# Pass by pass: the order of TensorE's products in a split-precision decoder trunk

## The chip, the cores and the metric

The kernel runs on one core of one Trainium2 chip. The metric is the device time of one execution in microseconds, as the median of several runs; less is better. The engines are named as in the profile: PE is TensorE's matmul stream, PEld its loading of weights, DVE, ACT and POOL are the vector, scalar and GpSimd engines, SP issues the transfers.

## The reference, cut to what matters

The input x has 256 tokens of width 1024. Two layers follow each other, and every large product is one of these lines:

```python
def swiglu(h, w_gate, w_up, w_down):
    return (jax.nn.silu(h @ w_gate) * (h @ w_up)) @ w_down        # 1024 -> 2816 -> 1024

# layer 0: half-step SwiGLU, Mamba-2 mixer, half-step SwiGLU
x = x + 0.5 * swiglu(rmsnorm(x, norm_w[0, 0]), w_gate[0, 0], w_up[0, 0], w_down[0, 0])
x = x + mamba2_mixer(rmsnorm(x, norm_w[0, 1]), ...)   # h @ w_in (1024 -> 5152), scan, y @ w_out (2048 -> 1024)
x = x + 0.5 * swiglu(rmsnorm(x, norm_w[0, 2]), w_gate[0, 1], w_up[0, 1], w_down[0, 1])
# shared keys and values from the stream after layer 0
k, v = hkv @ w_k + b_k, hkv @ w_v + b_v
# layer 1: half-step SwiGLU, windowed attention over k and v, half-step SwiGLU, final norm
x = x + 0.5 * swiglu(...)
x = x + swa_sink_attention(h, k_rot, v, w_q, b_q, sinks, w_o, b_o, cos, sin)
x = x + 0.5 * swiglu(...)
return rmsnorm(x, final_norm_w)
```

## The kernel before, in words

All weights are cut into **units** of 128 x 1024 numbers, stored in HBM in the order of use and loaded two at a time (one chunk, 1 MB) into a ring of four chunks. For each unit ACT rounds the raw weights to a high part `hi` (L144) and DVE takes the rest as a low part `lo` (L155); `Weights.ahead` keeps four units cut in advance of the one that PE uses. Activations are split in the same way: `xh` and `xl` lie side by side in one tile `xs[k]` for each of the eight row tiles k of 128 rows; a feed-forward's hidden tile is split into `hh` and `hl`. A product is then three products: high weights with high activations, high weights with low activations, and low weights with high activations.

PE runs six stages one after the other: feed-forward (0,0), the mixer, feed-forward (0,1), feed-forward (1,0), attention, feed-forward (1,1). The order of instructions on every engine is written out by hand in `run`, `ffn`, `ssm` and `att`, with a list of slots (`Slots`) for the work that goes between two units. A feed-forward takes gate f, up f and, from f = 4 on, down f - 4; the four last down units stand at its end, the last two of them merged in `tail`.

Three helpers put a unit on PE:

- `wide` (L362 in the profile; gate `g_f` and up `u_f` of a feed-forward, 22 of each for each of the four) takes 512 columns (`xh` and `xl` together) against `hi`, and 256 columns (`xh`) against `lo`: 16 matmuls for a unit. Either the two kinds alternate, row tile by row tile ("alternating" below), or, with `by_part`, all eight wide ones stand ahead of all eight narrow ones ("pass by pass"). Before the change the feed-forwards (0,1) and (1,0) run pass by pass from f = 1 on, (0,0) and (1,1) alternate, and f = 0 alternates everywhere.
- `rows` (L382; down `da_f`, the mixer's output `sa`, attention's output `aa`) makes three matmuls of 256 columns for each of eight output tiles: 24 for a unit. `high_first` chooses between the orders high-high, high-low, low-high (in the down products of (0,1) and (1,0), without the last two) and high-high, low-high, high-low (elsewhere; the first letter is the weight's part).
- `unit` (L349; the first gate, the mixer's inputs `sb`, keys `kab`, queries `q`) makes 24 matmuls of 256 columns, three for each row tile in turn. The very first gate and the mixer's 16 x units are written pass by pass instead: high-high, low-high, high-low, eight row tiles each.

The mixer's 41 input units stand in the order dt, then for each of four groups B, C and x and z in turn. The key units kA and kB stand in feed-forward (1,0) behind f = 5.

Of the kernel before, what the change touches and what calls it, by code (L numbers as in the profile page):

```python
# [17 lines left out]
T = 256  # L18
D = 1024
KT = D // P  # L20
# [195 lines left out]
class Trunk:  # L216
# [119 lines left out]
        nc.scalar.copy(rs, b[:, 0:256])  # L336
        return rs

    def unit(self, what, out, xh=None, xl=None, before=None):

        nc = self.nc
        xh = self.xh if xh is None else xh
        xl = self.xl if xl is None else xl
        hi, lo = self.W.next(what)
        passes = [(k, w, x) for k in range(KT) for w, x in ((hi, xh), (hi, xl), (lo, xh))]
        if self.W.pos == 1 or what[0] == "x":
            passes = [(k, w, x) for w, x in ((hi, xh), (lo, xh), (hi, xl)) for k in range(KT)]
        for n, (k, w, x) in enumerate(passes):
            nc.tensor.matmul(out, w[:, k * P : (k + 1) * P], x[k], start=n == 0, stop=n == len(passes) - 1)  # L349
        if before:  # L350
            before()
        self.tick()
# [16 lines left out]
        self.slots.run()  # L369
        self.W.ahead(self.NPART - 2)  # L370

    def rows(self, units, accs, first, last, done=None, high_first=False):

        nc = self.nc
        for j in range(KT):
            out = accs[j % 4][:, (j // 4) * T : (j // 4) * T + T]
            s = slice(j * P, (j + 1) * P)
            for n, ((hi, lo), hh, hl) in enumerate(units):
                f, e = first and n == 0, last and n == len(units) - 1
                passes = ((hi, hh), (hi, hl), (lo, hh)) if high_first else ((hi, hh), (lo, hh), (hi, hl))  # L380
                for m, (w, x) in enumerate(passes):
                    nc.tensor.matmul(  # L382
                        out, w[:, s], x, start=f and j < 4 and m == 0, stop=e and m == 2, skip_group_check=True
                    )
            if done:
                done(j, out)
# [90 lines left out]
    def ffn(self, l, i, key, nxt):  # L477
        nc, wk = self.nc, self.fw
        self.stage_norm(key)
        accs = self.accs(f"da_{key}")  # L480
        hs = {}

        def evac(f, g, u):
            hh = self.op.tile([P, T], F32R, tag="high", name=f"hh_{key}_{f}")
            hl = self.op.tile([P, T], F32R, tag="low", name=f"hl_{key}_{f}")
            hs[f] = (hh, hl)

            def e0():
                nc.vector.tensor_tensor(g, g, self.rs, ALU.mult)
                nc.scalar.activation(g, g, AF.Silu)  # L490
                nc.vector.tensor_tensor(u, u, self.rs, ALU.mult)

            def e1():
                nc.vector.tensor_tensor(u, u, g, ALU.mult)
                nc.scalar.activation(hh, u, AF.Copy)

            def e2():
                nc.vector.tensor_tensor(hl, u, hh.bitcast(F32), ALU.subtract)

            wait = max(0, 4 - f) if key == "f0" else 2 if f == 0 else 0  # L500
            self.slots.chain(wait, [e0, e1, e2])

        def product(name, f, t):

            b = self.bank(f"{name}_{key}_{f}")
            if self.W.pos == 0:
                self.slots.at(0, lambda: nc.scalar.copy(t, b[:, 0:T]))
                self.unit((name, l, i, f), b[:, 0:T])
                return

            def add():
                nc.scalar.copy(t, b[:, T:])  # L512
                nc.vector.tensor_tensor(t, b[:, 0:T], t, ALU.add)  # L513

            self.slots.at(0, add)
            self.wide((name, l, i, f), b, by_part=l != i and f > 0)

        for f in range(NF):
            g, u = (wk.tile([P, T], F32, tag=n, bufs=4, name=f"{n}s_{key}_{f}") for n in "gu")
            product("g", f, g)  # L520
            evac_now = lambda: evac(f, g, u)
            self.slots.late(0, evac_now)
            product("u", f, u)
            if l == 1 and i == 0 and f == 0:
                self.split_k()
            if l == 1 and i == 0 and f == 5:
                self.shared_k()
            if f >= LAG:
                self.down(l, i, f - LAG, hs, accs)
        for f in range(NF - LAG, NF - 2):  # L530
            self.down(l, i, f, hs, accs)
        self.tail([(("d", l, i, f), *hs.pop(f)) for f in (NF - 2, NF - 1)], accs, nxt)

    def down(self, l, i, f, hs, accs):
        hi_lo = self.W.next(("d", l, i, f))
        hh, hl = hs.pop(f)
        self.rows([(hi_lo, hh, hl)], accs, f == 0, False, high_first=l != i)
        self.tick()

    def tail(self, units, accs, nxt):  # L540
# [7 lines left out]
    def ssm(self, nxt):  # L548
# [9 lines left out]
        accs = []  # L558
# [11 lines left out]
        def half():  # L570
            if st["n"] % 2 == 0:
                st["bank"] = self.bank(f"sb{st['n']}")
            o = st["bank"][:, (st["n"] % 2) * T : (st["n"] % 2) * T + T]
            st["n"] += 1
            return o

        def conv(c, out, o, d):
            u = ubufs[st["u"] % 4]
            st["u"] += 1

            def c0():
                V.tensor_tensor(u[:, 3:], o, self.rs, ALU.mult)

            def c1():
                A.activation(out, u[:, 3:], AF.Identity, scale=self.s("convw", 3 * 24 + c), bias=self.s("convb", c))

            def c2():
                pairs = st["taps"]
                pairs.append((out, u, c))
                if len(pairs) == 1:  # L590
                    sl.late(0, taps)

            def c3():
                A.activation(out, out, AF.Silu)

            sl.chain(d, [c0, c1, c2, c3])
# [168 lines left out]
        def evac(what, o, d):  # L765
            kind = what[0]
            if kind == "dt":
                dt_chain(o, d)
            elif kind == "z":
                zs[what[1]] = z = wk.tile([P, T], F32, tag="zs", bufs=16, name=f"zs{what[1]}")  # L770
                sl.at(d, lambda: V.tensor_tensor(z, o, self.rs, ALU.mult))
                sl.at(d + 1, lambda: A.activation(z, z, AF.Silu))
            elif kind == "x":
                xs[what[1]] = x = wk.tile([P, T], F32, tag="xs", bufs=8, name=f"xs{what[1]}")
                conv(what[1], x, o, d)
            else:
                t = wk.tile([P, T], F32, tag=kind, name=f"{kind}{what[1]}")
                (B if kind == "B" else C)[what[1]] = t
                conv((16 if kind == "B" else 20) + what[1], t, o, d)
# [3 lines left out]
        at = {w: n for n, w in enumerate(seq)}  # L783
        ins = [w for w in seq if w[0] != "so"]

        E = {w: max(3, at[ins[min(i | 1, len(ins) - 1)]] + 1) for i, w in enumerate(ins)}
# [11 lines left out]
        for g in range(GROUPS):  # L798
# [7 lines left out]
            last = max(max(ymm_at[t // 2] + 1, E["z", t] + 2) for t in range(4 * g, 4 * g + 4))  # L806
# [8 lines left out]
            done = last + 3 + NORM_AT[g] + SCALE_AT[g]  # L815
# [7 lines left out]
        for what in seq[:-2]:  # L823
            if what[0] == "so":
                tt = what[1]
                if not accs:
                    accs = self.accs("sa")
                self.rows([(self.W.next(what), yh[tt], yl[tt])], accs, tt == 0, False)
                self.tick()
            else:  # L830
                o = half()
                self.unit(what, o, before=lambda: evac(what, o, E[what] - at[what]))
        self.tail([(w, yh[w[1]], yl[w[1]]) for w in seq[-2:]], accs, nxt)


# [69 lines left out]
    def att(self, nxt):  # L905
# [124 lines left out]
        for j in range(4):  # L1030
            if j == 3:
                vb = self.bank("vps")
                self.shared_v(0, vb)
                sl.at(0, lambda: vdone(vb))
                self.shared_v(1, vb)
            b = self.bank(f"q{j}")
            self.unit(("qA", j), b[:, 0:T])
            Q[j] = [wk.tile([P, T], F32, tag=f"Q{r}", name=f"Q{j}_{r}") for r in range(2)]

            def q_rope(j=j, b=b):  # L1040
                self.rope(b, self.rs, self.s("bq", 2 * j), self.s("bq", 2 * j + 1), "cosq", "sinq", Q[j], f"q{j}")

            d = 2 if j == 0 else 1
            sl.at(d, q_rope)
            d += 2
            sl.late(d, lambda j=j: scores(j))
            d += (4, 3, 3, 1)[j]
            sl.late(d, lambda j=j: turn(j))
            d += (0, 2, 2, 0)[j]
            sl.late(d, lambda j=j: pv(j))  # L1050
            self.unit(("qB", j), b[:, T:])
        accs = self.accs("aa")
# [182 lines left out]
```

## Time and profile before

| what | value |
|---|---|
| median of 3 runs | 1048.29 us (1047.95 to 1049.29) |
| time of the profiled execution | 1048.69 us |
| its span, first to last instruction | 1046.9 us |
| PE busy | 1025.2 us, 98% of the span |
| DVE, ACT, POOL busy | 775.1, 627.7, 79.4 us |
| matmuls, and weight loads | 7290 each |
| feed-forward (0,0), 7.30 to 201.70 | 194.40 us |
| mixer, 201.70 to 398.50 | 196.80 us |
| feed-forward (0,1), 398.50 to 581.60 | 183.10 us |
| feed-forward (1,0), 581.60 to 770.70, with the keys | 189.10 us |
| attention, 770.70 to 846.50 | 75.80 us |
| feed-forward (1,1) and the end, 846.50 to 1046.90 | 200.40 us |

PE is busy nearly all the time, but the profile's matmuls overlap, so that a busy PE can still be a slow one. What counts is the distance from one matmul's start to the next one's. The time of the execution is 1.8 us above the span.

### The profile page before, as it was taken

How to read it: one execution, taken by the hardware profiler on the slowest of the kernel's cores; microseconds unless marked ns; L12 is line 12 of the kernel's file. 1: busy time of each engine (PE TensorE's matmuls, PEld its weight loads, DVE VectorE, ACT ScalarE, POOL GpSimd, SP SyncE). 2: the span in 40 equal slices, each digit the busy share in tenths (PEclk: the TensorE clock that was granted, in tenths of full speed). 3: DMA queues.
4: the chain of work that ended last, by engine and by line, in shares of the span. 5: the costliest groups of instructions: out<-in, count | busy, mean ns of one | idle time of the engine just before them, and what ended most of it. 6: DMA issues, size and time to landing. Idle time of an engine off the chain costs nothing.

```text
span 1046.9 us, 18340 instructions
## 1 busy us (share of the span) xinstructions
PE 1025.2 (98%) x7290; PEld 948.2 (91%) x7290; DVE 775.1 (74%) x1420; ACT 627.7 (60%) x1106; POOL 79.4 (8%) x122
## 2 busy tenths in 40 slices
PE   8999999999999999999999999999999999999996
PEld 7899999999989898999999899999998888999996
DVE  4766666788999977766667796666689777666664
ACT  6555555669877756555555664555565766555554
POOL 3000000210110112000000200000031020000000
PEclk9999999999999999999999999999999999999998
DMA  8555554546545354555455455554554244555521
GB/s 304 195 201 176 186 200 164 194 171 252 217 156 213 131 201 153 197 201 200 169 203 200 157 211 200 177 209 178 202 202 152 92 161 167 196 186 191 187 101 40
DMA packets 30132, 190.84 MB, mean 182 GB/s; under 512 B 3904, under 2 KB 5728, under 8 KB 8544
## 3 DMA queue, kind: packets, MB, share of 16 engines
q1 hardware_dynamic: 30048, 189.69, 51.0%
q8 instruction: 57, 0.93, 0.4%
q14 instruction: 27, 0.22, 0.1%
HBM read 187.27 MB, written 1.10 MB: 180 GB/s over the span
## 4 chain that ended last, share of the span: by engine, by line
PE 80%; DVE 11%; ACT 3%; DMA 2%; POOL 1%; issue 1%; SPq 0%; ACTq 0%; DVEq 0%; POOLq 0%
PE u_f L362 23%; PE g_f L362 22%; PE da_f L382 22%; PE sa L382 3%; PE sb L349 3%; DVE lo L155 2%; DVE xs L394 2%; DMA csb<-cs_scratch 2%; PE aa L382 1%; PE q L349 1%; DVE xs L601 1%; DVE X L402 1%; DMA raw<-w 1%; DVE E L723 1%; ACT hi L144 1%
## 5 line engine op out<-in xcount | busy, mean ns | idle before, releaser
L155 DVE TENSOR_TENSOR lo<-raw,hi 128x1024 fp32r<-128x1024 f32 (+1 forms) x343 | 415.2, 1214 | 15.0 <-ACT hi L144 15.0
L144 ACT ACTIVATE hi<-raw 128x1024 fp32r<-128x1024 f32 (+1 forms) x343 | 357.3, 1047 | 18.9 <-PE da_f L382 5.1
L362 PE MATMUL u_f<-xs,hi 128*128 128x512 f32 x704 | 218.1, 397 | 0.0
L362 PE MATMUL g_f<-xs,hi 128*128 128x512 f32 x696 | 213.7, 395 | 0.8 <-DVE xs L394 0.8
L382 PE MATMUL da_f<-hh_f,hi 128*128 128x256 f32 x704 | 195.8, 278 | 0.0
L382 PE MATMUL da_f<-hh_f,lo 128*128 128x256 f32 x704 | 195.6, 278 | 0.0
L382 PE MATMUL da_f<-hl_f,hi 128*128 128x256 f32 x704 | 195.6, 278 | 0.0
L362 PEld LDWEIGHTS u_f<-xs,hi 128*128 128x128 f32 x704 | 130.1, 189 | 27.0
L362 PEld LDWEIGHTS g_f<-xs,hi 128*128 128x128 f32 x696 | 127.8, 188 | 27.2 <-DVE xs L394 2.2
L362 PE MATMUL u_f<-xs,lo 128*128 128x256 f32 x704 | 149.4, 280 | 0.0
L362 PE MATMUL g_f<-xs,lo 128*128 128x256 f32 x696 | 148.0, 281 | 0.0
L382 PEld LDWEIGHTS da_f<-hh_f,hi 128*128 128x128 f32 x704 | 132.3, 188 | 1.7
L382 PEld LDWEIGHTS da_f<-hl_f,hi 128*128 128x128 f32 x704 | 132.2, 188 | 0.0
L382 PEld LDWEIGHTS da_f<-hh_f,lo 128*128 128x128 f32 x704 | 132.1, 188 | 0.0
L513 DVE TENSOR_TENSOR gs_f<-g_f,gs_f 128x256 f32<-128x256 f32 x87 | 36.9, 424 | 113.7 <-ACT gs_f L512 113.6
L362 PEld LDWEIGHTS u_f<-xs,lo 128*128 128x128 f32 x704 | 114.1, 189 | 3.7
L362 PEld LDWEIGHTS g_f<-xs,lo 128*128 128x128 f32 x696 | 113.2, 188 | 3.3
L349 PE MATMUL sb<-xs,hi 128*128 128x256 f32 x656 | 108.0, 284 | 0.1
L513 DVE TENSOR_TENSOR us_f<-u_f,us_f 128x256 f32<-128x256 f32 x88 | 37.3, 424 | 88.8 <-ACT us_f L512 88.7
L512 ACT COPY us_f<-u_f 128x256 f32<-128x256 f32 x88 | 32.7, 371 | 111.4 <-PE u_f L362 111.3
L349 PEld LDWEIGHTS sb<-xs,hi 128*128 128x128 f32 x656 | 93.8, 190 | 1.2 <-issue 0.5
L512 ACT COPY gs_f<-g_f 128x256 f32<-128x256 f32 x87 | 32.1, 369 | 89.8 <-PE g_f L362 89.8
(252 smaller groups left out, 1369.4 us busy)
## 6 DMA issues: line engine op xcount, KB each, us to landing
raw<-w SPq DMA_DIRECT2D x168, 1024.0 KB, 4.9
csb<-cs_scratch SPq DMA_DIRECT2D x8, 768.0 KB, 7.0
raw<-w SPq DMA_DIRECT2D x4, 512.0 KB, 8.2
X<-x SPq DMA_DIRECT2D x4, 256.0 KB, 5.9
Q<-r_q SPq DMA_DIRECT2D x32, 32.0 KB, 1.9
out<-o SPq DMA_DIRECT2D x3, 256.0 KB, 2.2
ca<-const_att SPq DMA_DIRECT2D x1, 704.0 KB, 8.2
raw<-w SPq DMA_DIRECT2D x2, 256.0 KB, 5.2
```

The costliest lines, as they stand in the source:

```text
L144: self.nc.scalar.activation(hi[:, s], self.chunks[c][:, i, s], AF.Copy)
L155: self.nc.vector.tensor_tensor(lo[:, s], self.chunks[c][:, i, s], hi[:, s].bitcast(F32), ALU.subtract)
L349: nc.tensor.matmul(out, w[:, k * P : (k + 1) * P], x[k], start=n == 0, stop=n == len(passes) - 1)
L362: self.nc.tensor.matmul(out[:, 0:c], w[:, k * P : (k + 1) * P], x[k], start=n == 0, stop=n == len(passes) - 1, skip_group_check=True,)
L382: nc.tensor.matmul(out, w[:, s], x, start=f and j < 4 and m == 0, stop=e and m == 2, skip_group_check=True)
L394: nc.vector.scalar_tensor_tensor(self.xl[j], self.X[j], wcol(j), self.xh[j].bitcast(F32), ALU.mult, ALU.subtract)
L402: nc.vector.scalar_tensor_tensor(self.X[j], out, scale, self.X[j], ALU.mult, ALU.add)
L512: nc.scalar.copy(t, b[:, T:])
L513: nc.vector.tensor_tensor(t, b[:, 0:T], t, ALU.add)
L601: V.scalar_tensor_tensor(out, u[:, tap : tap + T], self.s("convw", tap * 24 + c), out, ALU.mult, ALU.add)
L723: V.tensor_tensor(f, f, c, ALU.mult)
```

## The change

`unit` now goes pass by pass for all its units, in the order high-high, high-low, low-high, except that the very first gate keeps its order and that two units (`fresh`: the mixer's dt and the first query) keep the three products of a row tile together. `ffn` asks `wide` for the pass-by-pass form in all four feed-forwards from f = 1 on. `rows` always takes the order high-high, high-low, low-high. No matmul is added or taken away, and the order on DVE, ACT, POOL and SP stays what it was.

```diff
-    def unit(self, what, out, xh=None, xl=None, before=None):
+    def unit(self, what, out, xh=None, xl=None, before=None, fresh=False):
...
-        passes = [(k, w, x) for k in range(KT) for w, x in ((hi, xh), (hi, xl), (lo, xh))]
-        if self.W.pos == 1 or what[0] == "x":
-            passes = [(k, w, x) for w, x in ((hi, xh), (lo, xh), (hi, xl)) for k in range(KT)]
+        first = self.W.pos == 1
+        parts = ((hi, xh), (lo, xh), (hi, xl)) if first else ((hi, xh), (hi, xl), (lo, xh))
+        passes = [(k, w, x) for w, x in parts for k in range(KT)]
+        if fresh:
+            passes = [(k, w, x) for k in range(KT) for w, x in parts]
...
-    def rows(self, units, accs, first, last, done=None, high_first=False):
+    def rows(self, units, accs, first, last, done=None):
...
-                passes = ((hi, hh), (hi, hl), (lo, hh)) if high_first else ((hi, hh), (lo, hh), (hi, hl))
+                passes = ((hi, hh), (hi, hl), (lo, hh))
...
-            self.wide((name, l, i, f), b, by_part=l != i and f > 0)
+            self.wide((name, l, i, f), b, by_part=f > 0)
...
-        self.rows([(hi_lo, hh, hl)], accs, f == 0, False, high_first=l != i)
+        self.rows([(hi_lo, hh, hl)], accs, f == 0, False)
...
-                self.unit(what, o, before=lambda: evac(what, o, E[what] - at[what]))
+                self.unit(what, o, before=lambda: evac(what, o, E[what] - at[what]), fresh=what == ("dt",))
...
-            self.unit(("qA", j), b[:, 0:T])
+            self.unit(("qA", j), b[:, 0:T], fresh=j == 0)
```

On PE, the gate unit of f = 5 in feed-forward (0,0) began like this before (`xs_84` to `xs_91` are the eight row tiles, `hi_423` and `lo_452` the two parts of one unit of weights):

```order
199 L362 MATMUL g_f_5_555<-xs_84,hi_423 128x512
200 L362 MATMUL g_f_5_555<-xs_84,lo_452 128x256
201 L362 MATMUL g_f_5_555<-xs_85,hi_423 128x512
202 L362 MATMUL g_f_5_555<-xs_85,lo_452 128x256
203 L362 MATMUL g_f_5_555<-xs_86,hi_423 128x512
204 L362 MATMUL g_f_5_555<-xs_86,lo_452 128x256
```

The same unit on PE after the change, where the seventh and eighth wide matmul meet the first narrow ones:

```order
205 L364 MATMUL g_f_5_555<-xs_90,hi_423 128x512
206 L364 MATMUL g_f_5_555<-xs_91,hi_423 128x512
207 L364 MATMUL g_f_5_555<-xs_84,lo_452 128x256
208 L364 MATMUL g_f_5_555<-xs_85,lo_452 128x256
209 L364 MATMUL g_f_5_555<-xs_86,lo_452 128x256
```

The eight narrow matmuls have moved from between the wide ones to behind them.

On PE, the first down unit of feed-forward (0,0) before (`da_f_205` and `da_f_206` are two of the output banks, `hh` and `hl` the split hidden tile):

```order
175 L382 MATMUL da_f_205<-hh_f_0_260,hi_393 128x256
176 L382 MATMUL da_f_205<-hh_f_0_260,lo_421 128x256
177 L382 MATMUL da_f_205<-hl_f_0_261,hi_393 128x256
178 L382 MATMUL da_f_206<-hh_f_0_260,hi_393 128x256
179 L382 MATMUL da_f_206<-hh_f_0_260,lo_421 128x256
180 L382 MATMUL da_f_206<-hl_f_0_261,hi_393 128x256
```

And after:

```order
175 L384 MATMUL da_f_205<-hh_f_0_260,hi_393 128x256
176 L384 MATMUL da_f_205<-hl_f_0_261,hi_393 128x256
177 L384 MATMUL da_f_205<-hh_f_0_260,lo_421 128x256
178 L384 MATMUL da_f_206<-hh_f_0_260,hi_393 128x256
179 L384 MATMUL da_f_206<-hl_f_0_261,hi_393 128x256
180 L384 MATMUL da_f_206<-hh_f_0_260,lo_421 128x256
```

Within each output tile the second and third product have changed places; the tile stays whole.

On PE, the key unit kA in feed-forward (1,0) before (`xkh` and `xkl` are the split activations for the keys, 16 tiles of their own):

```order
3989 L349 MATMUL kab<-xkh_6815,hi_7047 128x256
3990 L349 MATMUL kab<-xkl_6823,hi_7047 128x256
3991 L349 MATMUL kab<-xkh_6815,lo_7076 128x256
3992 L349 MATMUL kab<-xkh_6816,hi_7047 128x256
3993 L349 MATMUL kab<-xkl_6824,hi_7047 128x256
3994 L349 MATMUL kab<-xkh_6816,lo_7076 128x256
```

And after, at the seam of its first and second pass:

```order
4186 L351 MATMUL kab<-xkh_6820,hi_7047 128x256
4187 L351 MATMUL kab<-xkh_6821,hi_7047 128x256
4188 L351 MATMUL kab<-xkh_6822,hi_7047 128x256
4189 L351 MATMUL kab<-xkl_6823,hi_7047 128x256
4190 L351 MATMUL kab<-xkl_6824,hi_7047 128x256
```

The three products of one row tile now stand eight matmuls apart.

## Rows read from the trace of the kernel before

**Rows 1.** The page's busy times, and the granted clock of PE in 40 slices.

```profile
PE 1025.2 (98%) x7290; PEld 948.2 (91%) x7290; DVE 775.1 (74%) x1420; ACT 627.7 (60%) x1106; POOL 79.4 (8%) x122
...
PEclk9999999999999999999999999999999999999998
```

**Rows 2.** PE's waits over the span, first and last of 13: total us, times, longest.

```profile
PE st_yg L334 <- DVE dg_yg L329: 3.4, 3, 1.8
...
PE s L919 <- DVE m L934: 0.2, 1, 0.2
```

**Rows 3.** Timeline of PE in (0,0), alternating: first matmul of gate, up, down, gate.

```profile
46.17 0.40 PE L362 MATMUL g_f<-xs,hi 128*128 128x512 f32 x1
...
49.00 0.39 PE L362 MATMUL u_f<-xs,hi 128*128 128x512 f32 x1
...
51.83 0.28 PE L382 MATMUL da_f<-hh_f,hi 128*128 128x256 f32 x1
...
54.66 0.40 PE L362 MATMUL g_f<-xs,hi 128*128 128x512 f32 x1
```

**Rows 4.** Timeline of PE in (0,1), pass by pass: gate, up, down, next gate.

```profile
422.52 1.99 PE L362 MATMUL g_f<-xs,hi 128*128 128x512 f32 x8
424.35 1.11 PE L362 MATMUL g_f<-xs,lo 128*128 128x256 f32 x8
425.29 2.00 PE L362 MATMUL u_f<-xs,hi 128*128 128x512 f32 x8
...
428.04 0.28 PE L382 MATMUL da_f<-hh_f,hi 128*128 128x256 f32 x1
...
430.75 1.99 PE L362 MATMUL g_f<-xs,hi 128*128 128x512 f32 x8
```

**Rows 5.** Windows: length, busy PE, PEld, DVE, ACT, POOL; clock, DMA share, GB/s.

```profile
417.01:581.60 164.59, 164.59 (x1138) 152.10 (x1137) 116.62 (x193) 92.48 (x150) 2.34 (x3) 1.00 0.56 199
32.04:201.70 169.66, 169.66 (x1139) 155.82 (x1137) 118.03 (x196) 93.31 (x153) 2.45 (x4) 1.00 0.54 191
414.27:581.60 167.33, 167.33 (x1154) 154.51 (x1153) 118.62 (x197) 94.46 (x154) 2.34 (x3) 1.00 0.55 196
862.71:1035.20 172.49, 172.49 (x1155) 158.30 (x1153) 115.06 (x194) 90.37 (x148) 0.00 (x0) 1.00 0.44 156
```

**Rows 6.** Timeline of PE in (0,1), alternating f = 0 up unit, then f = 1.

```profile
403.10 0.39 PE L362 MATMUL u_f<-xs,hi 128*128 128x512 f32 x1
...
405.54 2.01 PE L362 MATMUL g_f<-xs,hi 128*128 128x512 f32 x8
```

**Rows 7.** Timeline of PE in the mixer: unit x0, then units z9 and x10.

```profile
212.84 1.10 PE L349 MATMUL sb<-xs,lo 128*128 128x256 f32 x8
213.78 1.34 PE L349 MATMUL sb<-xs,hi 128*128 128x256 f32 x10
...
289.52 0.39 PE L349 MATMUL sb<-xs,hi 128*128 128x256 f32 x2
...
291.90 1.07 PE L349 MATMUL sb<-xs,hi 128*128 128x256 f32 x8
292.81 1.07 PE L349 MATMUL sb<-xs,lo 128*128 128x256 f32 x8
```

**Rows 8.** Window over the two key units in (1,0).

```profile
619.49:625.25 5.76, 5.76 (x51) 5.76 (x50) 5.76 (x10) 3.97 (x7) 0.00 (x0) 1.00 0.60 222
```

**Rows 9.** Timeline of PE behind the keys: the down unit, then a gate unit.

```profile
625.25 0.28 PE L382 MATMUL da_f<-hh_f,hi 128*128 128x256 f32 x1
...
628.08 2.00 PE L362 MATMUL g_f<-xs,hi 128*128 128x512 f32 x8
```

**Rows 10.** Window in the mixer at the lower clock.

```profile
306.16:309.57 3.41, 3.41 (x18) 3.25 (x16) 1.72 (x6) 3.38 (x6) 2.38 (x5) 0.50 0.32 72
```

**Rows 11.** DMA issues: the weights' chunks, count, KB each, us to landing.

```profile
raw<-w SPq DMA_DIRECT2D x168, 1024.0 KB, 4.9
```

**Rows 12.** Waits of SP's queue, the longest: chunk loads waiting for a free buffer.

```profile
SPq L134 <- DVE lo L155: 702.6, 124, 11.0
```

## The prediction, on record before the changed kernel ran

> **What bounds the kernel now.** I read the page's busy times first: PE has 1025.2 us of a 1046.9 us span, DVE three quarters of it, ACT less [rows 1]. The table of PE's waits comes next. Its longest line is 3.4 us and its thirteen lines sum to 11.6 us [rows 2], so neither weights nor vector work hold PE up for long: TensorE's own stream is the bound, and only a shorter distance between two matmuls' starts can shorten the kernel by much. The busy times can't show that distance, since neighbouring matmuls overlap; the timeline's start times can.
>
> So I laid two stretches of that timeline side by side. In feed-forward (0,0), where wide and narrow matmuls alternate, a gate unit, an up unit and a down unit take 2.83 us each (46.17 to 49.00 to 51.83 to 54.66), 8.49 us in all [rows 3]. In feed-forward (0,1), which already runs pass by pass, the same three units take 2.77, 2.75 and 2.71 us, 8.23 us in all [rows 4]. The granted clock is 1.00 in both, which is the 2.4 GHz level [rows 5]. Columns, weights' sizes and instruction counts are the same. The trace of before thus holds the changed form beside the unchanged one, and whole stages can be compared.
>
> Finer: in the pass-by-pass stage the eight wide matmuls start 229 ns apart (1.83 us over 8) and the narrow ones 113 to 118 ns [rows 4]; a down unit has 2.71 / 24 = 113 ns per matmul there and 2.83 / 24 = 118 ns in (0,0) [rows 3, 4]. I call these the 113 and the 118 pace.
>
> **The change part by part.** Nothing is added or removed; only PE's order moves, so every term is a difference in PE's pace.
>
> *Feed-forward (0,0).* From the third gate after the first (g3) to the end of the last down unit it takes 169.66 us; (0,1) takes 164.59 us for the same units [rows 5]. Difference 5.07 us. Ahead of g3 lie a wait and a stretch at half clock, where I count only the up unit u2, at 2.83 - 2.75 = 0.08 us [rows 3, 4].
>
> *Feed-forward (1,1).* From u2 to the last down unit 172.49 us against 167.33 us in (0,1) [rows 5]: 5.16 us. Its g1, u1 and g2 add 0.06 + 0.08 + 0.06 = 0.20 us. Together with (0,0): 5.07 + 0.08 + 5.16 + 0.20 = 10.51 us.
>
> Is it the order, or the stage's place and data? Within (0,1) the f = 0 up unit still alternates: seven pairs from 403.10 to 405.54 take 349 ns each [rows 6], while a wide and a narrow one of the later units take 229 + 113 to 118 ns, 342 to 347 [rows 4]. One stage, one set of tiles, so the order does at least part of it. (0,0)'s pairs take 2.83 / 8 = 354 ns [rows 3]; alternating units thus come at more than one pace, and the f = 0 unit explains only half. I take the whole stage difference all the same, since (0,1) holds the pass-by-pass pace for 160 us.
>
> *The down units' own order.* About half of the 10.5 us comes from the down units, 44 times 0.12 us, yet their own new order may not be what earns it: the last four down units of (0,1) and the last ones of (1,0) keep 113 although their last two are written in the old order. I read it so that a pace, once set, is handed on from unit to unit, and that a pass of eight wide matmuls sets the 113 pace. The keys show it from the other side: behind them a down unit, in the new order already, takes 2.83 us (118 ns), and 113 is back after one pass-by-pass gate [rows 9]. Every down unit of the two feed-forwards stands behind such a unit after the change.
>
> *Keys.* kA and kB alternate over separate tiles and take 5.76 us, 120 ns per matmul [rows 8]. They are entered at the 113 pace. Pass by pass I expect them to keep it, as x10 did, pass by pass, behind z9 at 113 [rows 7]: 48 x 113.3 = 5.44 us, a gain of 0.32, and 0.12 on the down unit behind. The bounds are 5.76 (no gain) and 5.44; I take 5.44.
>
> *Mixer and attention.* Their 256-column units show no price of the order: x0 goes pass by pass at (213.78 - 212.84) / 8 = 118 ns, among neighbours that alternate at 118; z9 alternates at 113 (21 matmuls from 289.52 to 291.90), and x10 behind it, pass by pass, has 113 too [rows 7]. In the timeline 65 of these two stages' 73 units run at 118 and the rest at 113; the pace seems to be drawn anew where small matmuls stand between two units, and then kept. So I put B, C, z, q and the output units at zero. Bounds: all 65 at 113 would give 65 x 24 x 4.5 ns = 7.0 us; the 31 units that newly go pass by pass at the keys' 120 would cost 31 x 24 x 2.2 ns = 1.6 us.
>
> *Waits.* A low part is now needed later in its unit (after 8 wide, or 16 narrow matmuls, 1.8 to 1.9 us), `hl` one matmul earlier, long after it was made (down f - 4 stands behind up f); none of PE's thirteen waits names `lo` or `hl` today. In the x units `lo` is released eight matmuls (0.94 us) later, into a ring of six with four cut ahead: DVE doesn't meet it. DVE and ACT needed 117 and 92 us of the 165 us in (0,1) [rows 5], so they follow the shorter stage. What hides their work is PE itself; were that cover gone, it would show as waits in the first table.
>
> *Sum.* 10.51 + 0.32 + 0.12 = 10.95 us. The profiled execution took 1048.69 us, its span of 1046.9 and 1.8 around it; less 10.95 that is 1037.7. The median of the runs lies 0.4 lower, so I predict 1037.3 us.
>
> **The rivals.**
>
> *The mixer and attention catch the 113 pace too.* The stage is now entered at 113, and there are more passes. For it: z9 and x10 [rows 7]. Against: the other x units went pass by pass and stayed at 118, and waits for DVE in the mixer [rows 2] would eat a part. With half to all of the 7.0 us: 1030.3 to 1033.8 us.
>
> *Gates and ups gain, down units don't.* If (0,0) and (1,1) keep 118 in their down units, 44 x 0.12 + 0.12 = 5.4 us are lost from the sum: 1042.7 us. Against it: all down units of (0,1) and (1,0) but the one behind the keys.
>
> *No change.* Distances hang on columns alone and differ by stage for some other reason: 1048.3 us. For it: x0 and its alternating neighbours [rows 7]. Against: the f = 0 unit [rows 6]. The Trainium skill's page TensorE: Matmul & The Clock Gate, section Back-to-back issue gap, gives a warm gap that depends on the number of columns only, N/2.4 + 2.5 ns; by that rule the change would be worth nothing. The trace doesn't agree: 256 columns cost 113 or 118 ns at one clock [rows 3, 4].
>
> *Slower: weights come late.* The place is (0,0) and (1,1). A chunk carries two units and would be due every 8.23 x 2/3 = 5.49 us instead of 5.66. It lands 4.9 us after its issue [rows 11]. If loads couldn't keep 5.49, PE would wait; at 5.66 the gain is gone, and above that each 0.1 us costs 66 x 0.1 = 6.6 us: 5.76 would give 1054.9 us. Against: (0,1) took its chunks at 199 GB/s with a DMA share of 0.56 [rows 5], and the loads mostly wait for a buffer that DVE must free, 702.6 us in all [rows 12], not the other way round.
>
> **How the numbers follow.** Forecast 0.72; mixer and attention too 0.10; gates and ups only 0.08; no change 0.04; slower 0.02; the remaining 0.04 is a mixture. A stretch at half clock costs about 1.5 us (16 weight loads in 3.41 us, 213 instead of 118 ns each [rows 10]); one more or less of these, a few mixer units at another pace (2 us down, 1.6 up) and the keys' bound (0.4 up) make the range of the forecast 1034.0 to 1040.5, and with 0.76 to 0.8 in it that is also the range given. About 0.2% (2 us) is what can be told from no change here. Slower by more: 0.02; within it: 0.04; faster: 0.94.
>
> **What would show it.** In the changed profile, gate, up and down units of (0,0) and (1,1) at 2.77, 2.75 and 2.71 us from f = 2 on; g3 to the end of (0,0) near 164.6 us; the two keys at 5.44 us and the down unit behind them at 2.72; mixer and attention within 2 us of 196.8 and 75.8; PE's table of waits as short as before. The prediction is wrong if down units stay at 2.83, if PE waits for `hi`, `lo` or `raw`, or if the mixer's units settle at another pace.

## The result, and the profile after

The changed kernel takes 1038.8 us (median of 4 runs, 1038.29 to 1039.76) against 1048.79 us of the kernel before (median of 4 runs, 1047.95 to 1050.14): a ratio of 0.9905, 95% interval 0.9887 to 0.9922. It is faster by 10 us, about 1%. The profiled execution took 1038.29 us, its span is 1036.5 us, so 1.8 us lie around the span as before.

The page of the changed kernel, busy times and granted clock, answers to [rows 1]:

```profile
PE 1013.4 (98%) x7290; PEld 939.2 (91%) x7290; DVE 774.7 (75%) x1420; ACT 627.4 (61%) x1106; POOL 79.5 (8%) x122
...
PEclk9999999999999999999999999999999999999998
```

PE fell by 11.8 us, while the vector engines stayed within 0.4. The clock stands at the 2.4 GHz level nearly all the time in both, and in the stretches that earn the gain (below) it is 1.00 before and after, so the gain isn't a clock's.

The first lines of the table of PE's waits of the changed kernel (total us, times, longest), and the two on attention's scores:

```profile
PE st_yg L334 <- DVE dg_yg L329: 5.0, 4, 2.0
PE g_f L351 <- ACT hi L144: 1.5, 2, 0.9
...
PE s L921 <- DMA Q<-r_q: 0.7, 2, 0.6
PE s L921 <- DVE nm L942: 0.5, 1, 0.5
```

It has thirteen lines again, which sum to 13.6 us against 11.6; none names `raw` or `lo`. The two waits for `hi`, 1.5 us, lie in the very first gate, within 11 us of the start; the kernel before has one of 0.9 us there, so they do not come from a changed order. The longest line is where the mixer's norm waits for DVE, as in [rows 2], and its 1.6 us are most of the 2.0 us by which the sum grew.

Windows of the changed kernel, one for each stage that the prediction speaks of (length; busy PE, PEld, DVE, ACT, POOL with their counts; clock, DMA share, GB/s). In order: (0,0) from g3 on, (1,1) from u2 on, the mixer, (0,1), (1,0), attention.

```profile
31.77:196.37 164.60, 164.60 (x1138) 152.08 (x1137) 117.77 (x196) 93.14 (x153) 2.34 (x3) 1.00 0.56 196
857.82:1025.16 167.34, 167.34 (x1155) 154.49 (x1153) 114.91 (x194) 90.43 (x148) 0.00 (x0) 1.00 0.46 162
196.37:393.50 197.13, 190.78 (x1607) 184.63 (x1605) 173.50 (x332) 146.17 (x260) 30.07 (x53) 1.00 0.53 191
393.50:576.56 183.06, 182.81 (x1244) 167.92 (x1243) 130.53 (x218) 103.98 (x172) 7.10 (x11) 1.00 0.54 190
576.56:765.66 189.10, 188.84 (x1293) 173.80 (x1291) 138.64 (x234) 108.76 (x182) 9.75 (x14) 1.00 0.54 191
765.66:841.73 76.07, 73.57 (x620) 67.26 (x619) 65.64 (x188) 49.05 (x130) 16.32 (x20) 1.00 0.40 140
```

The first two answer to [rows 5]: 169.66 became 164.60, and 172.49 became 167.34. With the starts and ends of the stages, the 10.40 us by which the span fell are: (0,0) 5.33, (1,1) with the end 5.63, (0,1) 0.04; against them the mixer is 0.33 longer and attention 0.27, and (1,0) with the keys did not move at all. The mixer of the kernel before, for comparison:

```profile
201.70:398.50 196.80, 192.13 (x1606) 185.84 (x1605) 173.41 (x332) 146.20 (x260) 29.91 (x52) 0.99 0.53 191
```

Its clock of 0.99 is the stretch at half clock of [rows 10], which the changed kernel does not have in this stage. That earned nothing: in the changed kernel PE runs the unit at that place in less time and then waits 1.54 us for DVE, the new part of the longest line of waits above.

The timeline of PE in (0,0) of the changed kernel answers to [rows 3]:

```profile
45.53 1.99 PE L364 MATMUL g_f<-xs,hi 128*128 128x512 f32 x8
47.35 1.11 PE L364 MATMUL g_f<-xs,lo 128*128 128x256 f32 x8
48.30 2.00 PE L364 MATMUL u_f<-xs,hi 128*128 128x512 f32 x8
50.13 1.07 PE L364 MATMUL u_f<-xs,lo 128*128 128x256 f32 x8
51.04 0.28 PE L384 MATMUL da_f<-hh_f,hi 128*128 128x256 f32 x1
...
53.76 1.07 PE L364 MATMUL g_f<-xs,hi 128*128 128x512 f32 x4
```

Gate, up and down take 2.77, 2.74 and 2.72 us, as in (0,1) [rows 4]. A detail matters below: the gate's narrow pass still has 118 ns per matmul (0.94 to 0.95 us for eight), and only the up's has 113 (0.91 us); the down unit then keeps 113.

The keys in the changed kernel's timeline, with the down unit behind them:

```profile
614.45 1.12 PE L351 MATMUL kab<-xkh,hi 128*128 128x256 f32 x8
615.40 1.12 PE L351 MATMUL kab<-xkl,hi 128*128 128x256 f32 x8
616.36 1.12 PE L351 MATMUL kab<-xkh,lo 128*128 128x256 f32 x8
617.32 1.12 PE L351 MATMUL kab<-xkh,hi 128*128 128x256 f32 x8
...
620.20 0.28 PE L384 MATMUL da_f<-hh_f,hi 128*128 128x256 f32 x1
...
623.03 0.40 PE L364 MATMUL g_f<-xs,hi 128*128 128x512 f32 x1
```

Pass by pass the two units still take 5.75 us (5.76 in [rows 8]), 120 ns per matmul, and the down unit 2.83. This is the part of the forecast that did not come.

### The profile page after: what moved, and what is told of

It is laid out like the page before. It is cut to its first block, busy times and chain, and to the rows that moved or that the text cites. A ratio compares the mean times of both kernels' runs of the same rounds, so it can differ in the third digit from the quotient of the medians.

```text
span 1036.5 us, 18344 instructions
## 1 busy us (share of the span) xinstructions
PE 1013.4 (98%) x7290; PEld 939.2 (91%) x7290; DVE 774.7 (75%) x1420; ACT 627.4 (61%) x1106; POOL 79.5 (8%) x122
## 4 chain that ended last, share of the span: by engine, by line
PE 80%; DVE 12%; ACT 3%; DMA 2%; POOL 1%; issue 1%; SPq 0%; DVEq 0%; POOLq 0%
PE u_f L364 23%; PE g_f L364 22%; PE da_f L384 22%; PE sa L384 3%; PE sb L351 3%; DVE lo L155 2%; DVE xs L396 2%; PE aa L384 1%; DMA csb<-cs_scratch 1%; PE q L351 1%; DVE xs L603 1%; DVE X L404 1%; ACT hi L144 1%; DVE E L725 1%; ACT E L720 1%
## 5 line engine op out<-in xcount | busy, mean ns | idle before, releaser
L364 PE MATMUL u_f<-xs,hi 128*128 128x512 f32 x704 | 181.2, 395 | 0.0
L364 PE MATMUL g_f<-xs,hi 128*128 128x512 f32 x696 | 176.6, 392 | 0.8 <-DVE xs L396 0.8
L364 PEld LDWEIGHTS u_f<-xs,hi 128*128 128x128 f32 x704 | 127.1, 188 | 22.4
L364 PEld LDWEIGHTS g_f<-xs,hi 128*128 128x128 f32 x696 | 124.5, 188 | 23.9 <-DVE xs L396 2.2
L364 PEld LDWEIGHTS u_f<-xs,lo 128*128 128x128 f32 x704 | 95.6, 189 | 7.3
L364 PEld LDWEIGHTS g_f<-xs,lo 128*128 128x128 f32 x696 | 95.4, 188 | 6.7
L364 PE MATMUL g_f<-xs,lo 128*128 128x256 f32 x696 | 99.6, 280 | 0.0
L364 PE MATMUL u_f<-xs,lo 128*128 128x256 f32 x704 | 99.6, 278 | 0.0
L351 PE MATMUL sb<-xs,hi 128*128 128x256 f32 x656 | 87.0, 283 | 0.3 <-DVE xs L396 0.3
L351 PEld LDWEIGHTS sb<-xs,hi 128*128 128x128 f32 x656 | 80.9, 188 | 1.4 <-issue 0.5
```

The source lines that it names most:

```text
L364: self.nc.tensor.matmul(out[:, 0:c], w[:, k * P : (k + 1) * P], x[k], start=n == 0, stop=n == len(passes) - 1, skip_group_check=True,)
```

## The experiments

Two questions were open: which of the changed orders earns the gain, and what holds the keys at 120 ns. The theories are named in the expectations by letters. **A**: a pass of eight wide matmuls sets the 113 pace, and the units behind hand it on whatever their own order. **B**: each order earns its own part. **C**: the paces come from where operands begin, and operands that begin at multiples of 64 bytes are read faster. **D**: the pace hangs on the distance, modulo some power of two, between the addresses of the activations and of the weights in a partition.

**Experiment 1, the wide units alone.** The kernel before with one edit; the down, key, query and mixer units keep their old orders.

```diff
-            self.wide((name, l, i, f), b, by_part=l != i and f > 0)
+            self.wide((name, l, i, f), b, by_part=f > 0)
```

> Only the gate and up units of feed-forwards (0,0) and (1,1) go pass by pass; down units, keys, mixer and attention keep the order of before. Theory A (a pass of eight wide matmuls sets the 113 ns pace and the units behind it keep it, whatever their own order): the down units of both stages fall from 2.83 to 2.72 us although their order is the old one, and the whole gain is there, about 10.4 us less than before. Theory B (each product order earns its own part): only gates and ups gain, 2 x 2.9 = 5.8 us, and the down units stay at 2.83 us.

Measured: 1039.29 us (1038.14 to 1040.64), ratio to before 0.9911 (0.9896 to 0.9925), span 1036.4 us. Its window over (0,0) from g3 on:

```profile
31.38:195.99 164.61, 164.61 (x1139) 152.09 (x1137) 117.99 (x197) 93.34 (x154) 2.34 (x3) 1.00 0.57 198
```

That is the changed kernel's 164.60, down units included, though these keep high-high, low-high, high-low. (1,1) from u2 on takes the changed kernel's 167.34 as well:

```profile
857.30:1024.64 167.34, 167.34 (x1155) 154.50 (x1153) 114.94 (x194) 90.51 (x148) 0.00 (x0) 1.00 0.47 162
```

So all that these two stretches gain, 10.2 of the 10.4 us, comes from this one line of the change. B falls.

**Experiment 2, the down units' order alone.** The kernel before, `rows` always in the new order.

```diff
-                passes = ((hi, hh), (hi, hl), (lo, hh)) if high_first else ((hi, hh), (lo, hh), (hi, hl))
+                passes = ((hi, hh), (hi, hl), (lo, hh))
```

> Only the order of the three products in down, mixer-output and attention-output units is the new one; gates and ups of (0,0) and (1,1) alternate as before. Theory A: the pace handed on by alternating units is 118 ns, the down units stay at 2.83 us, and the time stays within 1 us of before. Theory B: the 44 down units gain 0.11 us each, about 5 us less than before.

Measured: 1049.17 us (1047.57 to 1050.82), ratio 1.0001 (0.9991 to 1.001). The same window:

```profile
30.37:200.03 169.66, 169.66 (x1139) 155.79 (x1138) 118.14 (x197) 93.55 (x154) 2.46 (x4) 1.00 0.55 192
```

169.66 us, to the hundredth what [rows 5] had. For the pace of the down units this order is worth nothing.

It does show in one other place, behind the last matmul of the down units, where the final norm follows. First the kernel before, then experiment 2:

```profile
1035.20 1.89 PE L451 MATMUL fin<-last_sq,ones 128*128 128x256 f32 x8
1040.23 2.77 DVE L465 TENSOR_TENSOR o<-last,fin 128x256 f32<-128x256 f32 x8 [0.47 <-ACT last L456]
...
1034.43 1.89 PE L451 MATMUL fin<-last_sq,ones 128*128 128x256 f32 x8
1039.10 2.77 DVE L465 TENSOR_TENSOR o<-last,fin 128x256 f32<-128x256 f32 x8
```

From the first line to the second it is 5.03 us before and 4.67 here, since DVE no longer waits ahead of the output. All 14 traces divide alike: from the start of the last down matmul to the end of the span it is 11.82 to 11.85 us in the six kernels with the old order in `rows`, and 11.46 to 11.48 in the eight with the new one. So this edit seems to be worth 0.36 us at the end of the program, too little for the times to tell; how it does so is not shown.

**Experiments 3 and 4, all large operands at multiples of 64 bytes**, in the changed kernel and in the kernel before. In both kernels `xs`, `hi`, `lo`, `hh`, `hl` and the keys' tiles begin 32 bytes behind a multiple of 64. Two unused tiles of 32 bytes end that:

```diff
+        top.tile([P, 8], F32, name="pad_top")
...
+        cp.tile([P, 8], F32, name="pad")
```

> The changed kernel with two unused pads of 32 bytes per partition, which move every operand of the large products from an address 32 bytes past a multiple of 64 to a multiple of 64 (read from the built program). Order and count of instructions are the same. Theory A says nothing of addresses: same time as the changed kernel, 1038 to 1039 us, keys at 120 ns. Theory C (the paces are counts of 64-byte pieces: 256 columns of 4 bytes at 2.4 GHz are 106.7 ns or 16 pieces, and the measured 113.3, 117.8 and 120 ns are 17, 17.7 and 18 of these): with aligned operands the matmul of 256 columns falls below 113 ns, towards 107 to 110, the keys leave 120, and the kernel gains 2 to 5%, 985 to 1017 us.

> The kernel of before with the same two pads. Theory A: within 1 us of before, alternating stages at 118 ns, pass-by-pass stages at 113. Theory C: 2 to 5% faster than before, and the difference between alternating and pass-by-pass stages, 5.1 us for a feed-forward, shrinks to under 2 us or is gone, since nothing crosses a 64-byte boundary.

Measured: the changed kernel 1053.71 us (1053.51 to 1055.72), ratio to before 1.0052 (1.0037 to 1.0067); the kernel before 1054.35 us (1052.65 to 1054.49), ratio 1.005 (1.0035 to 1.0065). Two empty tiles cost the changed kernel 15 us, and in sum the order is worth next to nothing any more. C falls: in (0,0) of the changed kernel gate, up and down take 2.80, 2.79 and 2.83 us. So where operands lie can cost more than the order earns.

In its parts the order still counts. PE in (0,0) of experiment 4, where gates and ups alternate: down, gate, up, down, gate.

```profile
59.74 0.28 PE L384 MATMUL da_f<-hh_f,hi 128*128 128x256 f32 x1
...
62.47 0.39 PE L364 MATMUL g_f<-xs,hi 128*128 128x512 f32 x1
...
65.30 0.40 PE L364 MATMUL u_f<-xs,hi 128*128 128x512 f32 x1
...
68.11 0.28 PE L384 MATMUL da_f<-hh_f,hi 128*128 128x256 f32 x1
...
70.94 0.39 PE L364 MATMUL g_f<-xs,hi 128*128 128x512 f32 x1
```

Gates and ups take some 2.82 us. Of the down units, every second one takes 2.72 to 2.73 (113 ns per matmul) and the next 2.83, as long as gates and ups stand between them. On average the three units together take 8.42 us here and 8.43 in experiment 3, where all 22 down units of the stage take 2.83. So at these addresses it is the alternating units that leave some down units at 113, and the pass-by-pass ones leave all at 118: what A says of the two orders does not hold here.

**Experiments 5 to 8, the weights moved**, in the changed kernel. One unused tile ahead of the pool of `hi` and `lo` moves these and all tiles behind them, the keys' tiles too, by 32, 64, 128 or 192 bytes; `xs`, `hh` and `hl` stay. For 32 bytes (for the others 16, 32 and 48 in place of 8):

```diff
+        shift = ctx.enter_context(tc.tile_pool(name="shift", bufs=1))
+        shift.tile([P, 8], F32, name="shift")
```

> The changed kernel with one unused pad that moves both weight parts (hi, lo) by 32 bytes per partition, so that the distance from the moving operands (xs, hh, hl) to the weights is 32 instead of 64 modulo 256 bytes. Theory D: the pace hangs on that distance, since every stretch that held 120 ns so far had a distance of 0 modulo 256 (the keys in all kernels, the mixer with both pads), and 113 or 118 belong to 64. At 32 a pace between 113 and 120 or one of the two: 1038 to 1054 us. Theory A alone: same as the changed kernel, 1038 to 1040 us.

> As the run before with 64 bytes: distance 0 modulo 256 for the feed-forwards, the mixer's input and output units and the queries. Theory D: all of these at 120 ns, down units 2.88 us as well, about 1055 to 1065 us. Theory A alone: 1038 to 1040 us.

> As before with 128 bytes: distance 192 modulo 256. Theory D has no row for this distance; if some distance lets two streams of reads never meet, the matmul of 256 columns falls to the 106.7 ns that its columns need at 2.4 GHz, a kernel of 985 to 1000 us; if 192 mirrors 64, 113 and 118 as in the changed kernel, 1036 to 1042 us. Theory A alone: 1038 to 1040 us.

> As before with 192 bytes: distance 128 modulo 256. Theory D: if the pace repeats every 128 bytes, 120 ns as at 0 (1055 to 1065 us); if 128 is the distance farthest from 0, a pace below 113 ns and under 1030 us. Theory A alone: 1038 to 1040 us.

Measured, one run each of 5 to 8 (the kernel before took 1050.54 beside them). The table gives the distances that follow from the addresses in the built programs: the address of the activations in a partition less that of the weights, modulo 128 bytes. Times of kernels and units are in us; gate, up and down are units of (0,0), from the timelines:

```
kernel                      xs  hh,hl  keys    us       gate   up     down        one key unit
after                       64   64     0    1038.8    2.77   2.74   2.72        2.88
7, weights + 128            64   64     0    1038.73   2.77   2.77   2.72        2.86, 2.88
5, weights + 32             32   32     0    1054.3    2.81   2.81   2.83        2.88
3, pads                      0   64     0    1053.71   2.80   2.79   2.83        2.88
6, weights + 64              0    0     0    1058.1    2.79   2.79   2.88        2.88
8, weights + 192             0    0     0    1059.57   2.80   2.80   2.85        2.86, 2.88
```

Moving by 128 bytes gives the changed kernel's time back; moving by 64 and by 192 are the two worst. The timeline of experiment 6 in (0,0):

```profile
44.47 2.00 PE L366 MATMUL g_f<-xs,hi 128*128 128x512 f32 x8
46.31 1.12 PE L366 MATMUL g_f<-xs,lo 128*128 128x256 f32 x8
47.26 2.00 PE L366 MATMUL u_f<-xs,hi 128*128 128x512 f32 x8
49.10 1.11 PE L366 MATMUL u_f<-xs,lo 128*128 128x256 f32 x8
50.05 0.28 PE L386 MATMUL da_f<-hh_f,hi 128*128 128x256 f32 x1
...
52.93 0.40 PE L366 MATMUL g_f<-xs,hi 128*128 128x512 f32 x1
```

Its down unit, with `hh` now at distance 0, takes 2.88 us, 120 ns per matmul: the keys' pace. And the keys, whose distance is 0 in all six kernels, have 119 to 120 in all six. So D, with a period of 128 bytes in the main.

The period is not exact. With the weights 128 bytes further (experiment 7) up units take 2.77 us instead of 2.74, while the mixer is 2.28 us shorter (194.85 against 197.13); at the two places of distance 0 down units take 2.88 and 2.85. Nor does a distance give one pace: in experiment 5 down units take 2.83 us in (0,0) and (1,0) and 2.80 in (0,1) and (1,1), and in experiment 4, where `hh` and `hl` lie at 64 as in experiment 3, both 2.72 and 2.83 occur.

**Experiments 9 and 10, the keys moved.** D says that the keys' 120 ns is a matter of their place. One unused tile of 64 bytes ahead of the key tiles sets their distance to 64; the other tiles that it moves are not read by PE in this stage. Once in the changed kernel, once in the kernel before.

```diff
             self.V = kp.tile([P, 2, T], F32, name="V")
+            kp.tile([P, 16], F32, name="kpad")
```

> The kernel after with one unused 64-byte tile ahead of the 16 key tiles xkh and xkl, so that their distance to the weights changes from 0 to 64 bytes modulo 128, like that of xs and hh; nothing else that PE reads moves. Theory D (the pace hangs on that distance): kA and kB at 113 ns, 5.44 to 5.5 us instead of 5.75, and the down unit behind them at 2.72 to 2.75 instead of 2.83; time 0.3 to 0.5 us less than after, near 1038.4. Rival (the keys are slow by their 16 separate tiles of 256 columns, which PE reads one after the other): 5.75 and 2.83 again, 1038.8.

> The same 64-byte tile in the kernel before, where kA and kB alternate. Theory D with theory A (a pace that was set is handed on whatever the order): the keys are entered at 113 and keep it, 5.44 to 5.5 us instead of 5.76, and the down unit behind them takes 2.72; the span falls by 0.4 us to 1046.5. Rival (at the good distance too, alternating keys fall back to 118): 5.66 us and 2.83.

Measured: experiment 9 takes 1038.6 us (1036.95 to 1041.25), ratio to before 0.9917 (0.9895 to 0.994), span 1035.9; experiment 10 takes 1048.47 us in one run, beside 1047.96 of before, span 1046.7. The times can't tell 0.4 us, the timelines can. Experiment 9:

```profile
614.13 1.07 PE L351 MATMUL kab<-xkh,hi 128*128 128x256 f32 x8
615.03 1.07 PE L351 MATMUL kab<-xkl,hi 128*128 128x256 f32 x8
...
619.57 0.28 PE L384 MATMUL da_f<-hh_f,hi 128*128 128x256 f32 x1
...
622.29 0.39 PE L364 MATMUL g_f<-xs,hi 128*128 128x512 f32 x1
```

The window over the two keys in experiment 10, where they alternate:

```profile
619.62:625.06 5.44, 5.44 (x50) 5.44 (x49) 5.44 (x10) 3.66 (x7) 0.00 (x0) 1.00 0.56 203
```

5.44 us in both, 48 times 113.3 ns, and the down unit behind them 2.72. The order of the keys is worth nothing in either place; 64 bytes are worth 0.42 us (8.58 us less 8.16 from the first key to the next gate). It is the distance and not the keys' own address: in experiment 6 they begin at the very same address as here and take 120 ns, with the weights at 96 bytes modulo 128 there and at 32 here. Nor is it the weights' address alone, which is the same in experiment 9 as in the changed kernel.

**Experiments 11 and 12, fewer pass-by-pass units.** How far is a pace handed on? The kernel of experiment 1 with only the gates, and with only f = 1, pass by pass.

```diff
-            self.wide((name, l, i, f), b, by_part=f > 0)
+            self.wide((name, l, i, f), b, by_part=name == "g" and f > 0)
...
-            self.wide((name, l, i, f), b, by_part=f > 0)
+            self.wide((name, l, i, f), b, by_part=f == 1)
```

> The kernel before, with the pass-by-pass order for the gate units alone (f > 0, all four feed-forwards); all up units alternate, also in (0,1) and (1,0), and the down units keep their old order. Theory A in its strong form (the pass of eight wide matmuls sets the pace and every unit behind it hands it on, alternating ones too): up units near 2.75 us and down units 2.72 in all four stages, 1039 us. Rival (an alternating wide unit loses the pace each time): up and down units at 2.83, the three together 8.43 us; against before 42 times 0.06 us gained in (0,0) and (1,1) and 42 times 0.20 lost in (0,1) and (1,0), 1055 us.

> The kernel before, with the pass-by-pass order for one gate and one up unit of each feed-forward alone (f = 1); all others alternate. Theory A in its strong form: one such unit is enough and the pace is handed on through the whole stage, 1039 to 1040 us. Rival (alternating wide units lose the pace): all four stages at 8.49 us for gate, up and down, against before 42 times 0.26 us lost in (0,1) and (1,0), 1060 us.

Measured: 1053.85 and 1060.6 us in one run each, beside 1048.8 of the kernel before. The rival's times came, 1055 and 1060 us. PE in (0,0) of experiment 11: a pass-by-pass gate, an alternating up, a down unit, the next gate.

```profile
45.92 2.00 PE L362 MATMUL g_f<-xs,hi 128*128 128x512 f32 x8
47.76 1.11 PE L362 MATMUL g_f<-xs,lo 128*128 128x256 f32 x8
48.71 0.39 PE L362 MATMUL u_f<-xs,hi 128*128 128x512 f32 x1
48.94 0.28 PE L362 MATMUL u_f<-xs,lo 128*128 128x256 f32 x1
...
51.49 0.28 PE L382 MATMUL da_f<-hh_f,hi 128*128 128x256 f32 x1
...
54.32 0.40 PE L362 MATMUL g_f<-xs,hi 128*128 128x512 f32 x1
```

Gate 2.79, up 2.78, down 2.83; the rival had the up at 2.83, which is nearly so in (0,1) and (1,1) only, with 2.82. Theory A in its strong form falls. With `xs` at 64 bytes from the weights, down units hand a pace on, in either order; an alternating wide unit doesn't keep the 113, and one pass-by-pass gate does not bring it back: its narrow pass has 118 ns here as in the changed kernel, where it is the pass-by-pass up behind it that comes to 113. Gate and up together did it (experiment 1); an up alone was not tried.

## Why the prediction was right, and where it was not

**The sum.** 10.95 us were predicted off the span, 10.40 came. The difference of 0.55 is made of the keys' 0.44 that did not come, 0.33 and 0.27 lost in mixer and attention, 0.04 gained in (0,1), and 0.18 and 0.27 more than predicted in (0,0) and (1,1). These last two are luck, and they hide the keys' miss. The 0.18 lies before g3, which starts at 30.37 us in experiment 2 and at 32.04 before, two kernels that are the same up to there. The 0.27 is the 0.36 at the end of the program (experiment 2), for which the prediction had no term, less 0.08 missing before u2. The median lies another 0.9 higher: the forecast put it 0.4 under the profiled time, and it came 0.5 above it.

**Feed-forwards (0,0) and (1,1).** Taking the whole stage difference from (0,1) held to 0.01 us: 164.60 for 164.59, 167.34 for 167.33. Experiment 1 shows that the order of the wide units is the cause, so the doubt about the f = 0 unit, whose 349 ns explained only half, was rightly set aside. Why alternating pairs come at 349 ns in one place and at 354 in another stays open; experiment 11 has both 2.79 and 2.82 us for alternating ups.

**"A pace, once set, is handed on from unit to unit".** Right for the down units (experiments 1 and 2), whose own order does not change their pace. Too wide for the alternating wide units (experiments 11 and 12). And "a pass of eight wide matmuls sets the 113 pace" is too short: it took the passes of a gate and of an up, and `xs` at 64 bytes from the weights (modulo 128). At distance 0 and 32 the narrow matmuls of the same passes take 117 to 119 ns and the down units 2.80 to 2.88 us. The prediction's "113 is back after one pass-by-pass gate" [rows 9] was read from two lines that do not show it. In the kernel before, the narrow pass of that gate has 118 ns (0.94 us for eight), and 113 is back in the up behind it (0.90 us):

```profile
629.92 1.11 PE L362 MATMUL g_f<-xs,lo 128*128 128x256 f32 x8
630.86 2.00 PE L362 MATMUL u_f<-xs,hi 128*128 128x512 f32 x8
632.70 1.07 PE L362 MATMUL u_f<-xs,lo 128*128 128x256 f32 x8
633.60 0.28 PE L382 MATMUL da_f<-hh_f,hi 128*128 128x256 f32 x1
```

All changed stages had both, so the forecast did not suffer. Nor did it suffer from the addresses, which the prediction did not look at, since the stages that it compared have the same ones.

**Keys.** The term that failed, whole: 0.32 and 0.12. The prediction read the 120 ns of [rows 8] as a price of the order, and took x10 [rows 7], which reads other tiles, as a sign that a pass-by-pass unit keeps what it finds. Experiments 9 and 10 show what the 120 ns goes with: key tiles at distance 0. The bound of no gain, 5.76, was named and came (5.75).

**Mixer and attention, put at zero.** Right in size, with 0.6 us lost. In the mixer z9 and x10 now have 118 instead of 113, 0.21 us of the 0.33. Experiments 1 and 2 have them at 118 as well, with the old order of the mixer's input units, and experiments 10 and 12, in that old order too, at 113; so the new order of these units is not the cause, and what draws the pace there stays open. The forecast's range took one stretch at half clock more or less as 1.5 us; one less came, in the mixer, and a wait of 1.54 us for DVE took its place. In attention 0.22 of the 0.27 is the second group of scores, which took 2.54 instead of 2.32 us and shows in the waits as L921.

**The rivals.** No late weights: no wait of PE names `raw`, and (0,0) drew 196 GB/s at a DMA share of 0.56, near the 199 GB/s and 0.56 that (0,1) had [rows 5]. Down units did not stay behind. The mixer did not catch the 113 pace, but it can: in experiment 7, at the same distances modulo 128, seven of its input units and seven of its output units run at 2.72. The rule of an issue gap from columns alone, which the prediction took from the Trainium skill's page TensorE: Matmul & The Clock Gate, section Back-to-back issue gap, is given there for a single matmul by itself, and the prediction left that out. It would make an estimated 109 ns of 256 columns. For this stream of matmuls, each with its weight load, it does not hold, and the addresses contradict it too: 256 columns took 113.3, 117.8 and 120.0 ns at a clock of 1.00, for the same instructions at other addresses (experiments 7, 5 and 6).

## What to carry to other kernels

Where PE is busy throughout, read the distance of matmul starts unit by unit. If one stage already runs a form that another lacks, the difference of the two whole stages can be the forecast; here it held to 0.01 us. Before pricing an order by a slow unit, ask whether it differs in its place in memory as well. Here the offset between activations and weights was worth as much (21 us between experiments 9 and 8) as the order of all wide units (21 us between experiments 12 and 1); these pairs are not from the same chip, and the kernel before, run beside them, differed by up to 2.6 us. At the other offset at which both orders were run (experiments 3 and 4) the new order earned next to nothing in sum. So look at the addresses of activations and weights when a tuned kernel's allocations change: one unused tile of 32 bytes took the whole gain away (experiment 5).

## What the runs showed of the hardware that was not expected

- At full clock and with a weight load for each matmul, a matmul of 256 columns in the long stretches mostly comes at one of few paces. Where activations and weights lie 64 bytes apart (modulo 128), these are 113.3 and 117.8 ns; the units before have a part in which of the two holds, but do not settle it (z9 and x10 in the mixer). At distance 0 down and key units have 119 to 120 (118.7 in the down units of experiment 8); at 32, 117.8 or 116.7 in the down units of experiment 5. Why the distance counts is not shown by these runs, and distances between these steps were not tried.
- The Trainium skill's page SBUF — State Buffer, section Who interferes with whom, gives TensorE two independent read ports, one for the moving operand and one for the weights. If independent is taken to mean that neither read can slow the other, the distance between the two should be worth nothing. The trace doesn't agree with that reading: 64 bytes alone took 72 matmuls from 8.58 to 8.16 us (experiment 9). Whether the ports have a part in it is not shown.
- The best kernel of these runs is experiment 9, the changed kernel with the keys moved; its 0.42 us over the changed kernel is seen in the timeline and lies under what the times can tell.
